# Another order for the mixer's 627 steps

## The chip, the core and the metric

The kernel runs on one core of one Trainium2 chip. The time is device microseconds of one launch. TensorE (PE) does the matmuls, VectorE (DVE), ScalarE (ACT) and GpSimd (POOL) work beside it, and SyncE (SP) issues most DMAs. Each engine takes its instructions in the order in which they are written for it, and waits on semaphores for what others produce.

## What is computed

One encoder layer on x of 512 positions by 1024 channels, in float32: a half-step FFN, a mixer of a Fourier part (512 channels) and grouped-query attention (8 query heads, 2 key heads of 64), and a second half-step FFN. The part that the change concerns:

```python
h = rms_norm(x, mix_norm)
u = h @ w_in                       # fourier 512 | q 8x64 | k 2x64 | v 2x64
f_out = fourier_mixer(u[..., :512], fnet_w, fnet_b)
    # Re(DFT2 over positions and a group's 128 channels), then a 128x128 map, 4 groups
a_out = gqa_attention(u_q, u_k, u_v, q_norm, k_norm)
    # per-head RMSNorm and axial rotary on q and k, softmax over all 512 keys
x = x + concat([f_out, a_out]) @ w_out
```

## The kernel before

**Stages.** FFN 1, the mixer and FFN 2 follow each other; in the profile the mixer's first matmul starts at 331.27 us and its last product ends at 491.05. Most matmul operands are split into a high and a low part, so that a product is three matmuls (high x high, high x low, low x high; L185 for the turned form). The high part (a step `.h`, or `h...`) is a cast, as a rule on ACT, the low part (`.l`, or `l...`, L129) a subtraction on DVE.

**The mixer as a list of steps.** Each step is a named closure that issues its instructions on its engines; the string ORDER names all 627, and L1393 to L1395 call them one after the other under a manual schedule, so each of the five engines gets its instructions in just that order. Nothing else decides it. The steps by name:

- `wk.r`, `wq0.r` to `wq3.r`, `wv.r`, `f0.r` to `f3.r`, `fw.r`, `o0.r` to `o7.r`: load a weight tile (SP, L153) into one of three raw buffers; `.h` (ACT, or DVE for f0 and f1; L840) and `.l` (DVE) split it.
- `k.0` to `k.7`, `q0.0` to `q3.7`, `v.0` to `v.7`: the projections, eight chunks of three matmuls each.
- For k and each q: `.sq` (ACT, squares), `.pq` (PE, four transposes, L917), `.s0`, `.s1` (sum and power), `.sw` (ACT, scaled copy, L877 or L882), `.sd` (q1 to q3 alone: four swap DMAs on SP, L891), `.rc`, `.rs` (DVE, the rotation), `.h`, `.l`. `kp` are four transposes on PE for k, `vt`, `vp`, `vs` bring v to rows (`vp`: four transposes, L983).
- `f<h><c>.0`, `.1`: the Fourier projections (twelve 256-column matmuls each, L1020 to L1022), with `.u`, `.e`, `.h`, `.l` behind them; `map0`, `map1`, `d..`, `c..` are the transforms. `pos` (L1391) issues three DMAs on POOL's queue with their tables.
- `s<t><c>` (PE, L1217): the scores of query pair t (two heads, b = 0 and 1) for query block c, into two PSUM banks. `m<t><c>` (DVE, L1226) takes the maxima, `e<t><b><c>` (ACT, L1243) the exponential into the head tile `th<t><b>`, `g` and `n<t><b><c>` (ACT, L1279) the scaling by the sum.
- The way to the transposed head blocks. For t = 1 to 3: `t<t><b><k>` (four transposes on PE, L1256), `h` (ACT, L1261) and `l` (DVE). For t = 0 (BY_BLOCKS): `T<t><b><g>` (DVE transposes 32x32 pieces), `Z<t><b><g>` (SP stores the piece to DRAM, L1162), `z<t><b><g>` (SP loads it back in another order, L1169), `h` (ACT, L1183), `l` (DVE). A block 00 or 01 has four of each.
- `v<t><b><k>` (PE, L1290): the attended sum, two matmuls; `o...c`, `o...a` and `r..` close a pair.
- `y<d>.0` to `.7` (PE): the output product; `y<d>.x` (DVE, L1328) adds it to x, `.q` squares it (ACT), `.a` adds that to the norm's sum (DVE, L1339), `.h`, `.l` scale and split it for FFN 2.

**What else binds the order.** Eight PSUM banks, mix0 to mix7 (L813), are handed out by `bank_for` in the order in which they were given back by `read`: a step that takes a bank waits for the last reader of its former content. Which bank a step gets therefore depends on ORDER too. The head tiles have two buffers: th10 and th11 take over those of the blocks 00 and 01, so the first exponential into each waits until that block's four stores are done. The loads `z` go into two `pt` buffers.

Of the kernel before, what the change touches and what calls it, by code (L numbers as in the profile page):

```python
# [50 lines left out]
ORDER = """
wq1.r wq0.r wk.r cos wk.h wk.l wq2.r k.0 k.1 wv.r wq0.h wq3.r k.2 k.3 k.4 k.5 k.6 wq0.l k.7 n1.c k.sq wq1.h n1.m q0.0
k.pq k.s0 wq1.l wq2.h q0.1 q0.2 q0.3 wq2.l q0.4 q0.5 k.s1 kw q0.6 k.sw q0.7 q0.sq k.rc q0.sw kp q1.0 q0.pq q2.0 q1.1
q1.2 k.rs km q1.3 q0.s0 q1.4 wv.h k.h q1.5 q0.rc q1.6 q0.rs q0.h k.l q1.7 q0.l f0.r s00 wv.l q1.sw s02 q0.s1 wq3.h
q1.sq m00 m02 f2.r s01 q2.1 m01 v.0 e010 e012 e000 q1.pq g00 q2.2 q1.s0 q2.3 e002 pos s03 v.1 g02 q2.4 q1.sd v.2 e011
v.3 e001 f1.r n012 n000 m03 wq3.l e013 q1.s1 e003 q3.0 v.4 v.5 n002 q1.rc q2.5 g01 g03 n001 n003 n011 q1.rs q2.6 v.6
n010 T000 q1.h Z000 q3.1 T002 q3.2 T003 Z002 n1.p v.7 q1.l q2.7 Z003 n013 T013 s13 s11 T012 T010 vt T011 f0.h Z010
q2.sq T001 Z011 f0.l m11 s10 Z012 q2.sw Z001 e101 Z013 m13 fw.r q3.3 f1.h e103 e111 z011 q3.4 f00.0 q3.5 z010 q3.6
e113 q2.sd m10 q3.7 f1.l f2.h z012 q2.rc q3.sq z003 vp z013 e100 q3.sw f2.l f01.0 vs s12 f00.1 h011 g13 f02.0 h010
z002 m12 f02.1 o0.r e110 v.h f01.1 f03.0 e112 z000 z001 q2.pq q2.rs v.l l010 q3.rc q2.h g11 e102 h000 q2.l v010 q3.pq  # L60
f00.u l000 v000 f02.e n103 l011 h002 f3.r n101 f12.0 g12 f03.1 h001 v011 f10.0 g10 l002 l001 q3.sd v001 q2.s0 n100
f01.u n112 q3.rs f3.h n102 v002 t100 n111 h012 f3.l l012 n113 f10.1 h003 f02.h h013 q3.s0 l003 t102 n110 h100 f10.u
v003 t101 f03.e h102 q2.s1 v012 l013 v013 f03.h l100 o00.c f02.l f12.1 h101 o01.c t110 h110 v100 l102 o00.a q3.h l101
t112 v101 f12.e t103 v102 h112 s22 h103 o01.a q3.l l112 o2.r s23 l103 fw.h f12.h m23 l110 r0.h t111 m22 h111 v103 e203
e213 f03.l l111 f11.0 fw.l t113 g23 e202 f11.1 f11.u s21 s20 o10.c v110 e212 n203 n213 m21 f13.0 e201 h113 f13.1 m20
d10 e211 f12.l g21 f13.e e200 o10.a g22 map0 o1.r n201 e210 d00 f13.h map0.h n202 d01 g20 d0.h map1 n200 map1.h l113
r0.l d11 f13.l v111 map0.l t202 d0.l map1.l t200 v112 d1.h d1.l s32 h202 h200 n210 o0.h c0.c c0.s l202 t201 c0.q q3.s1
l200 m32 v113 o0.l n212 d20 o11.c o1.h c0.o c1.s h201 c1.q c0.h d21 d2.h o3.r c1.c o11.a n211 c1.o d30 s33 l201 v200
t203 v201 d2.l o2.h h203 e312 t210 m33 l203 v202 d31 c0.l t213 h210 l210 e313 v203 t211 d3.h h213 t212 d3.l l213 h211
c1.h l211 s31 e303 e302 v210 o5.r v211 m31 c2.s h212 g33 e301 e311 s30 l212 v212 m30 n303 o2.l y0.0 c2.q c1.l n313  # L70
c3.s c2.c e300 g31 g32 v213 e310 o20.c o1.l n301 y2.0 g30 y2.1 c2.o y0.1 n302 n300 y1.0 c2.h y1.1 o20.a t302 t301 c3.c
c3.q t300 n312 h302 c2.l h300 c3.o c3.h l300 y2.2 c3.l n311 o21.c y1.2 t303 r1.h n310 o21.a y0.2 v300 y0.3 r1.l y2.3
h303 h301 l303 t310 y2.4 l301 r2.h o4.r t313 y0.4 v301 l302 v302 h310 t311 v303 l310 t312 v310 o7.r h313 y1.3 h311
l311 o30.c l313 h312 o6.r v311 l312 y2.5 v312 v313 y0.5 y1.4 r2.l o31.c o30.a y1.5 o31.a y1.6 r3.h y0.6 r3.l y0.7 y1.7
o5.h o5.l o3.h y2.6 y2.7 y0.x y5.0 y5.1 y5.2 o4.h o3.l y3.0 y5.3 y5.4 y5.5 y3.1 y3.2 o4.l y3.3 y0.h y3.4 y4.0 y3.5
y5.6 y3.6 y4.1 y5.7 y2.x y2.q y2.h o6.h y0.q y5.x y4.2 o6.l y3.7 y4.3 y6.0 y1.x y4.4 y2.l y1.q y6.1 y1.h o7.h y6.2
y3.x y4.5 y4.6 y6.3 o7.l y1.a y4.7 y6.4 y0.l y5.h y6.5 y4.x y5.q y4.h y3.q y6.6 y7.0 y4.q y7.1 y7.2 y2.a y1.l y3.h
y6.7 y4.l y7.3 y3.a y7.4 y5.l y6.x y3.l y4.a y7.5 y5.a y7.6 y6.h y6.q y7.7 y6.a y7.x y7.q y7.h y6.l y7.a y7.l
"""


# [1546 lines left out]
```

## Time and profile before

| | us |
|---|---|
| runs | 823.25, 826.04, 826.79 (median 826.04) |
| the profiled execution | 825.55 |
| its span, first to last instruction | 823.8 |
| mean granted TensorE clock | 0.994 of full speed |
| the mixer, first matmul to last | 331.27 to 491.05 |
| the mixer's stretch at half clock | 387.33 to 394.16 |

The profile comes from one execution, and all times in the trace are counted from the span's start. Names in it leave out buffer numbers: `mix` is one of the eight banks, `th` a head tile, `pt` a block that has come back from DRAM, `ph` and `pl` its high and low part, `sw_q` the swapped half of a query, `raw_f` a raw weight tile. In lists of waits, "PE mix L1290 <- ACT ph L1183" means that a matmul of line 1290 into a bank sat idle until the ACT instruction of line 1183, which writes `ph`, had ended.

### The profile page before, as it was taken

How to read it: one execution, taken by the hardware profiler on the slowest of the kernel's cores; microseconds unless marked ns; L12 is line 12 of the kernel's file. 1: busy time of each engine (PE TensorE's matmuls, PEld its weight loads, DVE VectorE, ACT ScalarE, POOL GpSimd, SP SyncE). 2: the span in 40 equal slices, each digit the busy share in tenths (PEclk: the TensorE clock that was granted, in tenths of full speed). 3: DMA queues.
4: the chain of work that ended last, by engine and by line, in shares of the span. 5: the costliest groups of instructions: out<-in, count | busy, mean ns of one | idle time of the engine just before them, and what ended most of it. 6: DMA issues, size and time to landing. Idle time of an engine off the chain costs nothing.

```text
span 823.8 us, 13012 instructions
## 1 busy us (share of the span) xinstructions
PE 811.9 (99%) x4936; PEld 723.8 (88%) x4936; DVE 649.3 (79%) x1065; ACT 499.7 (61%) x864; POOL 67.1 (8%) x75
## 2 busy tenths in 40 slices
PE   9999999999999999998999999999999999999997
PEld 7889998799989998877987888889988998899987
DVE  7997997489856857787898488999955998479674
ACT  7883774168524745677899467657732774257562
POOL 0320000000000100210100002200000100000001
PEclk9999999999999999999999999999999999999999
DMA  7874543345443423458011226564442553445222
GB/s 256 198 176 166 152 121 90 122 129 166 90 154 103 115 53 115 145 203 210 27 52 52 78 77 166 115 192 147 116 123 95 154 162 77 140 129 133 69 78 102
DMA packets 39838, 103.95 MB, mean 126 GB/s; under 512 B 4704, under 2 KB 10976, under 8 KB 39776
## 3 DMA queue, kind: packets, MB, share of 16 engines
q1 hardware_dynamic: 30080, 86.80, 32.7%
q0 software_dynamic: 8832, 15.34, 11.0%
q8 instruction: 38, 0.62, 0.3%
q10 hardware_dynamic: 864, 0.98, 0.3%
q14 instruction: 24, 0.20, 0.1%
HBM read 95.51 MB, written 4.19 MB: 121 GB/s over the span
## 4 chain that ended last, share of the span: by engine, by line
PE 87%; ACT 5%; DVE 4%; DMA 2%; issue 1%; POOL 0%; SPq 0%; POOLq 0%; DVEq 0%; ACTq 0%
PE dn L185 24%; PE r L435 12%; PE r L440 8%; PE gu L185 7%; PE mix L185 6%; PE q L435 4%; PE q L440 4%; PE r L431 4%; PE p L431 4%; PE q L431 4%; PE gu L739 3%; ACT th L1243 2%; PE p L440 2%; PE mix L1290 1%; ACT th L1279 1%
## 5 line engine op out<-in xcount | busy, mean ns | idle before, releaser
L185 PE MATMUL dn<-at,ring 128*128 128x512 f32 x900 | 202.9, 380 | 1.1 <-DVE ring L129 1.1
L185 PEld LDWEIGHTS dn<-at,ring 128*128 128x128 f32 x900 | 168.0, 188 | 30.1 <-DVE ring L129 1.5
L440 PE MATMUL r<-rt,ring 128*128 128x256 f32 x560 | 154.3, 276 | 0.0
L435 PE MATMUL r<-rt,ring 128*128 128x256 f32 x840 | 147.1, 276 | 0.0
L435 PEld LDWEIGHTS r<-rt,ring 128*128 128x128 f32 x840 | 127.1, 188 | 1.6
L440 PEld LDWEIGHTS r<-rt,ring 128*128 128x128 f32 x560 | 105.1, 188 | 0.2
L390 ACT CAST ring<-s 128x1024 fp32r<-128x1024 f32 x70 | 73.5, 1051 | 35.8 <-PE r L435 16.5
L129 DVE TENSOR_TENSOR ring<-s,ring 128x1024 fp32r<-128x1024 f32 x70 | 85.3, 1218 | 12.3 <-ACT ring L390 10.2
L574 DVE SCALAR_TENSOR_TENSOR gx<-dn,gx 128x512 f32<-128x512 f32 x61 | 41.9, 688 | 62.2 <-PE dn L185 62.1
L171 ACT CAST ring<-raw_dn 128x768 fp32r<-128x768 f32 (+3 forms) x58 | 45.3, 784 | 70.2 <-PE dn L185 55.3
L440 PE MATMUL q<-rt,ring 128*128 128x256 f32 x280 | 77.0, 275 | 0.0
L159 POOL DMA_DIRECT2D ring<-in_wgu x38 | 32.9, 866 | 470.7 <-ACT u L449 340.5
L129 DVE TENSOR_TENSOR ring<-raw_dn,ring 128x768 fp32r<-128x768 f32 (+3 forms) x58 | 51.5, 891 | 9.2 <-ACT ring L171 4.8
L440 PEld LDWEIGHTS q<-rt,ring 128*128 128x128 f32 x280 | 52.6, 188 | 0.0
L129 DVE TENSOR_TENSOR ring<-raw_g,ring 128x1024 fp32r<-128x1024 f32 x35 | 42.7, 1220 | 9.9 <-PE p L431 9.6
L435 PE MATMUL q<-rt,ring 128*128 128x256 f32 x280 | 49.8, 277 | 0.0
L185 PE MATMUL gu<-ring 128*128 128x512 f32 x216 | 48.9, 381 | 0.0
L431 PE MATMUL r<-rt,ring 128*128 128x512 f32 x140 | 48.6, 383 | 0.0
L431 PE MATMUL q<-rt,ring 128*128 128x512 f32 x140 | 48.4, 382 | 0.0
L431 PE MATMUL p<-rt,ring 128*128 128x512 f32 x140 | 48.3, 382 | 0.0
L185 PEld LDWEIGHTS gu<-ring 128*128 128x128 f32 x216 | 40.4, 188 | 6.9
L390 ACT CAST ring<-raw_g 128x1024 fp32r<-128x1024 f32 x35 | 36.8, 1051 | 14.0 <-DMA raw_g<-in_wgu 11.0
(276 smaller groups left out, 1636.7 us busy)
## 6 DMA issues: line engine op xcount, KB each, us to landing
raw_g<-in_wgu SPq DMA_DIRECT2D x35, 512.0 KB, 3.9
raw_u<-in_wgu SPq DMA_DIRECT2D x35, 512.0 KB, 4.5
raw_dn<-in_wd SPq DMA_DIRECT2D x40, 384.0 KB, 3.2
ring<-in_wgu POOLq DMA_DIRECT2D x35, 256.0 KB, 4.4
raw_gu<-in_wgu SPq DMA_DIRECT2D x12, 512.0 KB, 3.4
raw_o<-in_wo SPq DMA_DIRECT2D x8, 512.0 KB, 3.4
raw_dn<-in_wd SPq DMA_DIRECT2D x8, 448.0 KB, 3.4
raw_wq<-in_wins SPq DMA_DIRECT2D x4, 512.0 KB, 3.3
```

The costliest lines, as they stand in the source:

```text
L129: nc.vector.tensor_tensor(out=lo, in0=src, in1=asf(hi), op=ALU.subtract)
L159: nc.gpsimd.dma_start(out=lo, in_=src, accum_op=ALU.add)
L171: nc.scalar.copy(hi[:, :n, :], raw[:, :n, :])
L185: nc.tensor.matmul(ps, a, b, start=first and b is mhi and a is whi, stop=last and a is wlo)
L390: nc.scalar.copy(hi, src)
L431: nc.tensor.matmul(turned(ps), whi[:, ks], turned(m), start=start, stop=False, skip_group_check=True)
L435: nc.tensor.matmul(ps[:, t], whi[:, ks], m[:, o * HALF :][:, t], start=start and o == 0, stop=False, skip_group_check=True,)
L440: nc.tensor.matmul(o, wlo[:, ks], m, start=False, stop=stop, skip_group_check=True)
L574: nc.vector.scalar_tensor_tensor(out=x[d][:, t], in0=ps[:, t], scalar=0.5, in1=x[d][:, t], op0=ALU.mult, op1=ALU.add)
L739: nc.tensor.matmul(turned(pss[c]), w[:, k % 2, c], turned(m[k]), start=k == 0 and m is hh and w is hi, stop=k == KD - 1 and w is lo,)
L1243: nc.scalar.activation(prob[t, b, c], scores, AF.Exp, bias=mxs[n][:, b : b + 1], scale=f[:, b : b + 1], accum_out=zs[t][:, c, b : b + 1],)
L1279: op(f"n{t}{b}{c}")(lambda b=b: nc.scalar.activation(prob[t, b, c], prob[t, b, c], AF.Copy, scale=z(b)))
```

## The change

Only the string ORDER differs. It names the same 627 steps, in another order from its first line to its last; no step's own code changes. Its first two lines and the line with block 00's last store, before and after:

```diff
-wq1.r wq0.r wk.r cos wk.h wk.l wq2.r k.0 k.1 wv.r wq0.h wq3.r k.2 k.3 k.4 k.5 k.6 wq0.l k.7 n1.c k.sq wq1.h n1.m q0.0
-k.pq k.s0 wq1.l wq2.h q0.1 q0.2 q0.3 wq2.l q0.4 q0.5 k.s1 kw q0.6 k.sw q0.7 q0.sq k.rc q0.sw kp q1.0 q0.pq q2.0 q1.1
...
-n010 T000 q1.h Z000 q3.1 T002 q3.2 T003 Z002 n1.p v.7 q1.l q2.7 Z003 n013 T013 s13 s11 T012 T010 vt T011 f0.h Z010
...
+wk.r wk.h wq0.r wv.r wk.l k.0 k.1 k.2 wq1.r k.3 wq0.h k.4 k.5 k.6 k.7 wq0.l n1.c q0.0 wq2.r cos k.sq wq3.r k.pq q0.1
+q0.2 k.sw q0.3 q0.4 n1.m f1.r f2.r q0.5 k.s0 q0.6 k.rc wq1.h wq1.l wq2.h q0.7 k.s1 kw kp q0.sw k.rs q1.0 q1.1 wq2.l
...
+Z002 q3.5 T000 q3.6 T012 vt s13 s10 Z013 Z012 T011 f1.h q2.rc m13 e103 s11 q3.7 Z000 m11 f1.l m10 q3.sw Z010 q3.sq
```

What this does to the engines is shown at three places. First SP's queue around the stores Z (out, L1162) and the loads z (pt, L1169) of the blocks 00 and 01; sw is the four swaps `.sd`, raw a weight load. A row is line, operation, what it writes and reads, and how often in a row. Before:

```order
L153 DMA raw_f2_3479<-in_winf 128x1024
L891 DMA sw_q1_3458<-own_q1_3459 32x512 x4
L153 DMA raw_f1_3545<-in_winf 128x1024
L1162 DMA out00_3588<-th00_3501 128x512 x3
L1162 DMA out01_3628<-th01_3498 128x512 x3
L1162 DMA out00_3588<-th00_3501 128x512
L1162 DMA out01_3628<-th01_3498 128x512
L153 DMA raw_fw_3658<-in_fw 128x512
L1169 DMA pt01_3667<-out01_3628 32x4x512 x2
L891 DMA sw_q2_3646<-own_q2_3647 32x512 x4
L1169 DMA pt01_3667<-out01_3628 32x4x512
L1169 DMA pt00_3710<-out00_3588 32x4x512
```

And SP after:

```order
L153 DMA raw_f0_3529<-in_winf 128x1024
L153 DMA raw_f3_3570<-in_winf 128x1024
L891 DMA sw_q2_3584<-own_q2_3585 32x512 x4
L1162 DMA out00_3622<-th00_3506 128x512 x3
L1162 DMA out01_3649<-th01_3511 128x512 x2
L1162 DMA out00_3622<-th00_3506 128x512
L1162 DMA out01_3649<-th01_3511 128x512 x2
L1169 DMA pt01_3721<-out01_3649 32x4x512 x4
L1169 DMA pt00_3780<-out00_3622 32x4x512 x2
L891 DMA sw_q3_3682<-own_q3_3683 32x512 x4
L153 DMA raw_fw_3848<-in_fw 128x512
L1169 DMA pt00_3780<-out00_3622 32x4x512 x2
```

The swaps of q2 moved from behind the stores to ahead of them, block 00's fourth store from seventh to sixth place, and the eight loads now follow the stores directly, with the swaps of q3 and fw ahead of the last two.

Second, ACT around the first exponentials of pair 1 (th10 and th11; mix are the banks of their scores, own_q2 and own_q3 the copies `.sw`). Before:

```order
L976 COPY vt_3624<-mix5_3293 128x512
L869 ACTIVATE sq_q2_3630<-mix7_3295 128x512
L877 ACTIVATE own_q2_3647<-mix7_3295,qkg_119 128x512
L1243 ACTIVATE th10_3651,z1_3650<-mix6_3294,mx11_3635,sc_3287 128x512
L1243 ACTIVATE th10_3651,z1_3650<-mix0_3288,mx13_3654,sc_3287 128x512
L1243 ACTIVATE th11_3665,z1_3650<-mix1_3289,mx11_3635,sc_3287 128x512
L1243 ACTIVATE th11_3665,z1_3650<-mix2_3290,mx13_3654,sc_3287 128x512
L840 CAST more_3283<-raw_f2_3479 128x1024
```

After:

```order
L877 ACTIVATE own_q2_3585<-mix7_3295,qkg_119 128x512
L1279 ACTIVATE th01_3511<-th01_3511,z0_3505 128x4x4x32 x2
L869 ACTIVATE sq_q2_3611<-mix7_3295 128x512
L976 COPY vt_3635<-mix3_3291 128x512
L1243 ACTIVATE th10_3661,z1_3660<-mix2_3290,mx13_3656,sc_3287 128x512
L877 ACTIVATE own_q3_3683<-mix4_3292,qkg_119 128x512
L869 ACTIVATE sq_q3_3686<-mix4_3292 128x512
L1243 ACTIVATE th11_3688,z1_3660<-mix6_3294,mx13_3656,sc_3287 128x512
L840 CAST more_3283<-raw_f2_3376 128x1024
```

The first exponential of pair 1 is now e103, reading mix2, and not e101; q3's copy and squares stand between it and the second one.

Third, PE where f00.0 (the first Fourier projection) ends. Before, the projection chunk q3.5 and vp follow:

```order
L1020 MATMUL mix7_3295<-ring_61 128x256
L1021 MATMUL mix7_3295<-ring_61 128x256
L1022 MATMUL mix7_3295<-ring_61 128x256
L185 MATMUL mix3_3291<-ring_61,more_3283 128x4x32x4 x9
L983 MATMUL mix6_3294<-ident_108,vt_3624 128x128 x4
```

After, f02.0 follows:

```order
L1020 MATMUL mix3_3291<-ring_61 128x256
L1021 MATMUL mix3_3291<-ring_61 128x256
L1022 MATMUL mix3_3291<-ring_61 128x256
L1020 MATMUL mix2_3290<-ring_61 128x256
L1021 MATMUL mix2_3290<-ring_61 128x256
```

The projection q3 is now finished ahead of f00.0, vp comes behind f03.0, and the step behind f00.0 takes mix2, the bank that e103 reads.

More of the change, by code (lines that the diff above doesn't have):

```diff
@@ L51 @@
 ORDER = """
-wq1.r wq0.r wk.r cos wk.h wk.l wq2.r k.0 k.1 wv.r wq0.h wq3.r k.2 k.3 k.4 k.5 k.6 wq0.l k.7 n1.c k.sq wq1.h n1.m q0.0
-k.pq k.s0 wq1.l wq2.h q0.1 q0.2 q0.3 wq2.l q0.4 q0.5 k.s1 kw q0.6 k.sw q0.7 q0.sq k.rc q0.sw kp q1.0 q0.pq q2.0 q1.1
-q1.2 k.rs km q1.3 q0.s0 q1.4 wv.h k.h q1.5 q0.rc q1.6 q0.rs q0.h k.l q1.7 q0.l f0.r s00 wv.l q1.sw s02 q0.s1 wq3.h
-q1.sq m00 m02 f2.r s01 q2.1 m01 v.0 e010 e012 e000 q1.pq g00 q2.2 q1.s0 q2.3 e002 pos s03 v.1 g02 q2.4 q1.sd v.2 e011
-v.3 e001 f1.r n012 n000 m03 wq3.l e013 q1.s1 e003 q3.0 v.4 v.5 n002 q1.rc q2.5 g01 g03 n001 n003 n011 q1.rs q2.6 v.6
@@ L57 @@
-n010 T000 q1.h Z000 q3.1 T002 q3.2 T003 Z002 n1.p v.7 q1.l q2.7 Z003 n013 T013 s13 s11 T012 T010 vt T011 f0.h Z010
[L58 to L76, printed above, removed]
@@ L77 @@
-y3.x y4.5 y4.6 y6.3 o7.l y1.a y4.7 y6.4 y0.l y5.h y6.5 y4.x y5.q y4.h y3.q y6.6 y7.0 y4.q y7.1 y7.2 y2.a y1.l y3.h
-y6.7 y4.l y7.3 y3.a y7.4 y5.l y6.x y3.l y4.a y7.5 y5.a y7.6 y6.h y6.q y7.7 y6.a y7.x y7.q y7.h y6.l y7.a y7.l
+wk.r wk.h wq0.r wv.r wk.l k.0 k.1 k.2 wq1.r k.3 wq0.h k.4 k.5 k.6 k.7 wq0.l n1.c q0.0 wq2.r cos k.sq wq3.r k.pq q0.1
+q0.2 k.sw q0.3 q0.4 n1.m f1.r f2.r q0.5 k.s0 q0.6 k.rc wq1.h wq1.l wq2.h q0.7 k.s1 kw kp q0.sw k.rs q1.0 q1.1 wq2.l
+q1.2 km q0.rc q1.3 k.h q1.4 k.l q1.5 q0.sq q0.rs q0.pq q1.6 wv.h q0.s0 q2.0 q0.h q1.7 q0.s1 q0.l wv.l wq3.h s00 q1.sw
@@ new lines @@
+m00 s01 s02 m01 q2.1 q2.2 q2.3 q1.sq q1.sd m02 wq3.l e000 q2.4 e010 q2.5 s03 g00 q1.rc e001 q2.6 f0.r e011 q2.7 g01
+e002 m03 e012 v.0 q1.pq n000 n011 n001 e013 q3.0 q3.1 q1.rs v.1 e003 g02 f0.h g03 f0.l n010 f3.r n002 q1.s0 n003 v.2
+q1.h T002 v.3 q2.sw n013 q1.l T001 T003 q3.2 n012 T013 q3.3 v.4 v.5 q1.s1 n1.p q2.sd q2.sq v.6 q3.4 v.7 Z001 T010 Z003
+Z002 q3.5 T000 q3.6 T012 vt s13 s10 Z013 Z012 T011 f1.h q2.rc m13 e103 s11 q3.7 Z000 m11 f1.l m10 q3.sw Z010 q3.sq
+e113 f00.0 q2.rs Z011 q3.rc f02.0 f2.h g13 z013 z010 e111 f00.1 f03.0 f2.l vp e101 e110 q3.pq vs z011 e100 z012 s12
@@ new lines @@
+h011 h012 v.h m12 v.l z001 l011 h010 f02.1 z003 g10 f00.u e112 q2.pq f01.0 q3.sd e102 l010 f02.e n110 f10.0 n100 v010
+v011 f3.h fw.r g11 z002 z000 n101 f03.1 q2.h q3.rs h013 q2.s0 h000 l012 f12.0 n103 g12 f3.l f01.1 l000 n113 q2.s1 n102
+q3.s0 f01.u v012 f03.e h002 o5.r t101 v000 n111 l013 t100 h001 q2.l f10.1 fw.h f03.h f10.u v013 l001 l002 f12.1 v001
+h003 v002 q3.h f03.l fw.l l003 f12.e t102 n112 h100 h101 l101 l100 o2.r v003 o01.c o00.c s22 s23 h102 o00.a o01.a v100
+l102 v101 pos t103 m22 t110 r0.h f02.h f11.0 h103 m23 f11.1 h110 e212 f12.h f11.u t112 f02.l v102 l103 e213 l110 t113
@@ new lines @@
+t111 h112 e203 o0.r v103 q3.l l112 s21 g23 e202 s20 f13.0 o10.c f13.1 n203 m21 h113 e211 o10.a map1 e201 m20 o2.h l113
+v110 e200 e210 o2.l d00 map1.h g21 f13.e o1.r map1.l n201 map0 h111 map0.h g22 d01 g20 d10 l111 d11 d0.h n202 d0.l
+v111 v112 n200 d1.h f13.h t200 v113 c0.s map0.l f12.l d1.l h200 c1.c f13.l o11.c c0.c c1.s c0.q l200 q3.s1 c0.o t201
+n210 o11.a d20 t202 n212 o3.r c1.q h201 d21 h202 c1.o n213 t203 d2.h v200 l201 l202 s33 h203 s32 d2.l n211 v201 l203
+c2.s t212 c0.h o0.h m33 m32 d30 d31 e313 t211 h212 c2.q d3.h c0.l e312 v202 h211 l212 c2.c v203 t210 t213 d3.l c2.o
@@ new lines @@
+s31 l211 h210 l210 c3.s m31 v210 e302 o0.l c1.h v211 c3.q c1.l s30 m30 o1.h v212 e311 e303 e301 y0.0 c2.h o1.l o6.r
+o4.r g31 g32 e310 h213 e300 l213 c2.l c3.c y0.1 g33 g30 y2.0 n301 n302 n303 y2.1 y1.0 y1.1 v213 r0.l y0.2 y2.2 y1.2
+n300 t301 c3.o t300 o20.c t302 o20.a t303 c3.h n311 c3.l y1.3 h300 y0.3 h301 n313 l300 h302 v300 l302 l301 h303 n310
+y1.4 y2.3 v301 n312 o21.c t310 o21.a h310 y2.4 t311 l310 t312 v302 t313 r1.h l303 r2.h v303 r1.l h311 v310 l311 v311
+h312 h313 o30.c l312 y0.4 l313 v312 o30.a v313 r2.l o31.c y2.5 o31.a y0.5 y2.6 r3.h y1.5 r3.l y1.6 y2.7 o5.h y1.7 y0.6
@@ L79 @@
+o5.l y0.7 y0.x y5.0 y5.1 o3.h o7.r y5.2 o3.l y3.0 y2.x y2.h y5.3 y2.q y3.1 y1.x y3.2 y5.4 y3.3 y2.l y5.5 y5.6 o6.h
+y5.7 y3.4 o4.h y1.h o4.l y3.5 y3.6 y3.7 y1.q y4.0 o6.l y0.q y5.x y4.1 y6.0 y3.x y6.1 y4.2 y4.3 y0.h o7.h y1.a y5.q
+y6.2 y4.4 y4.5 y2.a y6.3 y3.q y4.6 y4.7 o7.l y4.x y5.h y3.a y6.4 y1.l y4.q y0.l y6.5 y4.a y3.h y6.6 y6.7 y5.l y7.0
+y7.1 y6.x y7.2 y5.a y6.h y3.l y7.3 y6.l y6.q y7.4 y6.a y7.5 y4.h y7.6 y7.7 y7.x y4.l y7.q y7.a y7.h y7.l
 """
```

## The prediction

> **What bounds the kernel now.** I read the page's busy times first, then PE's list of waits, then PE's timeline at the longest wait, then the stretches around it.
>
> ```profile
> PE 811.9 (99%) x4936; PEld 723.8 (88%) x4936; DVE 649.3 (79%) x1065; ACT 499.7 (61%) x864; POOL 67.1 (8%) x75
> PE mix L1290 <- ACT ph L1183: 1.9, 1, 1.9
> PE mix L917 <- ACT th L1243: 1.2, 1, 1.2
> PE mix L1256 <- ACT th L1279: 0.5, 1, 0.5
> ```
>
> TensorE is busy for 811.9 of 823.8 us and has three waits of note (columns: total us, times, longest). All three lie in the mixer, which is the only stage that the change reorders; both FFNs keep their order. So the change can win what PE loses in the mixer, and no more, and it can lose whatever new waits it makes. The largest loss stands here:
>
> ```profile
> 383.73 0.60 PE L917 MATMUL mix<-ident,sq_q 128*128 128x128 f32 x4
> 384.59 0.49 PE L1290 MATMUL mix<-ph,near 128*128 128x512 f32 x1 [0.26 <-DVE near L129]
> 385.19 0.49 PE L1290 MATMUL mix<-pl,near 128*128 128x512 f32 x1
> 385.52 0.60 PE L917 MATMUL mix<-ident,sq_q 128*128 128x128 f32 x4
> 387.98 0.79 PE L1290 MATMUL mix<-ph,near 128*128 128x512 f32 x1 [1.86 <-ACT ph L1183]
> ...
> 337.65 0.60 PE L917 MATMUL mix<-ident,sq_k 128*128 128x128 f32 x4
> 338.00 4.90 PE L185 MATMUL mix<-ring 128*128 128x512 f32 x21
> ```
>
> Each row is start, length, instruction, and in brackets the idle time ahead and who ended it. The last two rows give unhindered rates: four transposes take 0.35 us start to start, and a 512-column matmul (4.90 - 0.38) / 20 = 0.226. From 383.73 to 387.98 PE did 2 x 0.35 + 2 x 0.226 = 1.15 us of work in 4.25 us: **3.1 us are lost** while v010 and v000 wait for the head blocks that return from DRAM. Then the clock falls:
>
> ```profile
> 387.98:394.16 6.18, 6.18 (x25) 5.65 (x26) 6.10 (x13) 6.18 (x11) 1.92 (x1) 0.50 0.05 13
> 394.16:400.00 5.84, 5.84 (x46) 5.47 (x45) 4.11 (x8) 3.97 (x8) 1.84 (x2) 1.00 0.27 91
> ```
>
> In the table by stretches (PE first, the granted clock third from the right) PE does 25 matmuls in 6.18 us at clock 0.50 and then 46 in 5.84 us at 1.00. At the later rate the 25 take 3.2 us: **another 3.0 us** that the wait left behind. The 1.2 us wait (q1.pq, 354.70) did not cost clock. So what the mixer can give back is about 1.2 + 3.1 + 3.0 + 0.5 = 7.8 us, under 1%.
>
> **What goes.** q1.pq now stands behind q2.7 and v.0, when the exponentials that hold its bank have long read it: -1.2. The head blocks' way (e, n, T, store Z, load z, h) ends earlier against PE: in the new order v010, v000 and their kin stand behind more f-products, and the loads z are no longer mixed with o0.r and f3.r. I follow them with rows:
>
> ```profile
> L1162 SPq DMA_DIRECT2D out<-th x5: 320/320/443, 367.4 to 369.5; - x5
> DMA to landing us min/median/max: 2.0/2.4/2.9
> L1169 SPq DMA_DIRECT2D pt<-out x8: 302/442/580, 370.7 to 377.7; - x8
> DMA to landing us min/median/max: 4.4/5.6/9.5
> 371.75 2.42 SPq L891 DMA_DIRECT2D sw_q<-own_q  x4
> ```
>
> The first of five stores issued at 367.4 lands 2.0 later, the last at 369.5 + 2.9 = 372.4: 0.75 us apart, so they queue up: the issues are 0.53 apart. The first of the eight loads lands at 370.7 + 4.4 = 375.1 and the last at 377.7 + 9.5 = 387.2; between them land seven loads, one weight load (o0.r) and four swaps, which I count as one since they are as large as one load: 12.1 / 9 = 1.34 each. In the new order all eight stores have landed by about 376 (worked out below); then come eight loads, four swaps and fw, ten times 1.34: the last load lands near 389.4. From e103 (at 374.6, below) to h000 ACT has 22 instructions, by these groups (count, busy time, mean ns):
>
> ```profile
> L1243 ACT ACTIVATE th<-mix,mx,sc 128x512 f32<-128x512 f32 x32 | 24.8, 783 | 4.8 <-DVE mx L1227 4.3 <-PE mix L1256 0.5
> L1279 ACT ACTIVATE th<-th,z 128x512 f32<-128x512 f32 x32 | 22.3, 728 | 0.0
> L840 ACT CAST ring<-raw_o 128x1024 fp32r<-128x1024 f32 x5 | 5.2, 1043 | 0.0
> L1183 ACT CAST ph<-pt 128x512 fp32r<-128x512 f32 x8 | 4.8, 616 | 5.4 <-DMA pt<-out 3.0 <-issue 1.4 <-PE mix L1290 1.0
> ```
>
> 8 exponentials (6.3), 4 steps h (2.5), 3 scalings (2.2), f2.h and f3.h (2.1), and 5 of some 0.6 (3.0) make 16.1 us; so ACT comes to h000 near 390.5, and PE to v000 after 392. Both waits go: **-3.1, and -3.0 with the clock**. The wait ahead of t302 goes too (-0.5: y0.0 to y2.1 and the scalings are re-dealt there). At the end:
>
> ```profile
> 487.59 3.46 PE L185 MATMUL mix<-near,ring 128*128 128x512 f32 x15
> 489.54 2.21 DVE L1339 TENSOR_TENSOR acc<-acc,sq 128x512 f32<-128x512 f32 x3
> 491.67 0.68 DVE L1328 TENSOR_TENSOR gx<-mix,gx 128x512 f32<-128x512 f32 x1
> ```
>
> The last product ends at 491.05, but y7.x starts at 491.67, behind three square sums that the new order does earlier. FFN 2's norm hangs on y7.x: -0.6. Sum of what goes: **-8.4 us**. If the cover fails (the last load lands after 391.5), v000 waits again; that is a rival below. I cost two moves at nothing: the step pos (three transfers on POOL's queue, at 348 in before) now starts near 390, behind the loads, and its first reader map1 stands some 20 us further on; and the first weight loads wk, wq0 and wv on SP's queue land beside FFN 1's last down products, as wq1, wq0 and wk did.
>
> **What comes.** The new place to wait is f02.0, the PE step that in the new order follows f00.0. It takes the PSUM bank of score block s13, which e103, the first exponential of query pair 1, frees on ACT. e103 writes a head buffer that is free only when block 00 has been stored: four stores, and the last of them, Z000, is the sixth of eight in SP's queue. Ahead of the stores SP now issues the four swaps q2.sd. In the order of before those stood behind the stores, and PE had q3.3 to q3.7 to do meanwhile. The rows:
>
> ```profile
> 349.72 1.22 DVE L129 TENSOR_TENSOR ring<-raw_wv,ring 128x1024 fp32r<-128x1024 f32 x1
> 352.48 1.28 ACT L1243 ACT_TABLE_LOAD   x1 [0.58 <-DVE mx L1227]
> 353.78 0.78 ACT L1243 ACTIVATE th<-mix,mx,sc 128x512 f32<-128x512 f32 x1
> 361.06 3.19 ACT L1279 ACTIVATE th<-th,z 128x512 f32<-128x512 f32 x5
> 364.12 0.63 ACT L939 CAST near<-rot_q 128x512 fp32r<-128x512 f32 x1
> 367.57 0.68 ACT L877 ACTIVATE own_q<-mix,qkg 128x512 f32<-128x512 f32 x1
> 371.85 0.78 ACT L1243 ACTIVATE th<-mix,mx,sc 128x512 f32<-128x512 f32 x1 [3.59 <-DVE mx L1227]
> 374.34 0.36 PE L1020 MATMUL mix<-ring 128*128 128x256 f32 x1
> ```
>
> - The first exponential started at 353.78. Its maximum m00 comes about 0.8 us later now, because k.sw and wq1.h stand on ACT ahead of what DVE needs, and DVE idles there and does wq2.l afterwards, a lows step of the length of wv.l here; bounds 0 and 1.2. So 354.6.
> - From there to q1.h ACT needed 364.12 - 353.78 = 10.34 for 8 exponentials and 7 scalings. Now 6 scalings precede it, one less at 3.19 / 5 = 0.64: 9.7. With q1.h 0.63 and q2.sw 0.68, q2.sw ends at 365.6.
> - SP needs 2.42 for q2.sd: the first store goes out at 368.1, the sixth 5 x 0.38 later at 370.0 (issues took 0.32 to 0.44).
> - The first lands 2.1 after its issue, at 370.2, the sixth 5 x 0.75 later at **374.0**; with the swaps still in the queue up to 375.2.
> - e103 takes 0.78: f02.0 can start at 374.8 to 376.0; I take 375.4.
> - PE arrives there earlier. In before it began f01.0 at 374.34, having done the same work plus vp (0.35) and waited 1.2, so 372.8; with fewer changes between kinds of matmul a little less, with new short waits ahead of kp, q0.pq and s00 (taken as 0.9, between 0 and q1.pq's 1.2) a little more: 373.0, give or take 0.5.
>
> So f02.0 waits **+2.4 us** (1.3 to 3.5), and ACT idles some 6 us ahead of e103. Behind e103 on ACT stand q3.sw, q3.sq, e113 and f2.h: f03.0, q3.pq and the exponentials of pair 1 wait with it. The clock then is at stake. It fell after idle of 0.26 and 1.86 us close together, and not after 1.2; at 2.4 I take it to fall and to cost what it cost before: **+3.0** (0 to 3.4). Short waits: kp, q0.pq, s00 +0.9; further down t101, s23, t200 and t210, where ACT's or DVE's durations, laid end to end along the new order, end 0.5, 0.9, 0.6 and 0.4 behind PE's: 2.4 in all. A PE that runs 3 us late at half clock swallows the first two, so +1.0 (0 to 2.4). Sum of what comes: **+7.3 us**.
>
> **Sum.** -8.4 + 7.3 = -1.1. The profiled run took 825.55 us, 1.75 more than its span, and lies 0.5 under the median of 826.04, inside the runs' 823.25 to 826.79. 825.55 - 1.1 = **824.5 us**: the wait and its half clock move from v000 to f02.0.
>
> The Trainium skill, "TensorE: Matmul & The Clock Gate", section "What's actually happening", lets the clock fall only after at least one idle window of about 3.4 us. By that rule f02.0's wait would leave the clock alone and the sum would be that of the first rival. This trace speaks against it: the clock fell after a longest idle stretch of 1.86 us.
>
> **Rivals.**
> 1. *The clock stays up behind f02.0.* If the wait is short (1.3) or split by the end of the stretch over which activity is counted, the 3.0 go, and t101 and s23 wait again (+1.4): 824.5 - 3.0 + 1.4 = 822.9. For it: 1.2 us was harmless. Against it: 1.86 was not. 17%.
> 2. *The new order does what a search with the right transfer times should:* block 00 lands in time and f02.0 hardly waits: 824.5 - 2.4 - 3.0 + 1.4 = 820.5. It needs the six stores to land by 372, so 0.36 apart; five of before's were 0.75 apart. 10%.
> 3. *Slower: two long waits.* The last load lands after 391.5, because loads, swaps and fw share the queue after the stores: 2 us later than I add up, as z001 did here when swaps came between (9.5 us from issue). Then h000, l000 and v000 wait as in before, some 1.5 us, and the clock falls a second time (+3.0): 829.0. The point is 391.5, and PE, slowed at f02.0, is likelier to be late itself. 9%.
> 4. The remaining 64% is the forecast, within 822.5 to 827.
>
> **How the numbers follow.** A measurement here tells about 0.5% (4.1 us) from no change. Faster by more: the second rival, a part of the first, and a new f02.0 wait at its lower bound, 0.18. Slower by more: part of the third and what I don't see, 0.09. Same: 0.73. The range takes in the first and second rival at the low end (820.5) and most of the third at the high end (828.5).
>
> **What would show it.** Right: PE's longest wait is f02.0 (L1020) for an exponential (ACT th L1243), ACT idles 5 to 7 us ahead of it, a stretch at 0.50 follows it, and v010 and v000 (L1290) wait for nothing. Wrong: f02.0 without a wait (the stores landed sooner), a full clock behind it, or L1290 waiting for ph L1183 as before. A PE wait at k.0 or map1 would show that the moves costed at nothing were not free.

## The result, and the profile after

The change makes the kernel faster, by more than was forecast: 817.78 us (817.47 to 818.53, 4 runs) against 825.15 (823.25 to 826.79, 4 runs), ratio 0.9913, 95% interval 0.9888 to 0.9938. On the chip of e5 the ratio was 0.9929 (0.9915 to 0.9942). One execution of before on that chip took 1680.56 us, twice the others, and no comparison uses it. The forecast was 824.5, in a range of 820.5 to 828.5, with 0.18 on faster: the time lies below the range.

The profiled execution took 818.53 us with a span of 816.8, 7.0 under the span of before. Its list of PE's waits (total us, times, longest):

```profile
PE dn L185 <- DVE ring L129: 1.0, 1, 1.0
PE busy L684 <- PEq L1611: 0.8, 1, 0.8
PE mix L1020 <- ACT th L1243: 0.7, 1, 0.7
PE gu L739 <- ACT ring L725: 0.4, 1, 0.4
PE mix L1256 <- ACT th L1279: 0.3, 1, 0.3
```

Of the mixer's waits two are left, L1020 (f02.0, as predicted, but 0.7 and not 2.4) and L1256 (t200, 0.3). L1290 behind ph and L917 behind th are gone. The chain ahead of f02.0, in the timelines of SP, ACT and PE (start, length, instruction, idle ahead):

```profile
365.59 2.41 SPq L891 DMA_DIRECT2D sw_q<-own_q  x4
368.10 4.67 SPq L1162 DMA_DIRECT2D out<-th  x8
...
353.31 1.28 ACT L1243 ACT_TABLE_LOAD   x1 [0.75 <-DVE mx L1227]
354.61 0.78 ACT L1243 ACTIVATE th<-mix,mx,sc 128x512 f32<-128x512 f32 x1
373.89 0.78 ACT L1243 ACTIVATE th<-mix,mx,sc 128x512 f32<-128x512 f32 x1 [5.00 <-DMA out<-th]
...
372.61 0.28 PE L1020 MATMUL mix<-ring 128*128 128x256 f32 x1
373.88 0.28 PE L1022 MATMUL mix<-ring 128*128 128x256 f32 x1
374.81 0.39 PE L1020 MATMUL mix<-ring 128*128 128x256 f32 x1 [0.66 <-ACT th L1243]
```

The swaps go ahead of the stores, ACT idles 5.0 us for a store, and then e103 lets f02.0 start: every link of the prediction up to there is found, with other sizes. e103 starts at 373.89, and PE comes to f02.0 near 374.0, one step of 0.11 behind the last matmul of f00.0. The half clock that was to follow does not come, and the stretch in which before had it runs at full speed (PE first, granted clock third from the right):

```profile
373.97:380.00 6.03, 5.37 (x46) 5.04 (x44) 5.91 (x12) 6.03 (x14) 0.00 (x0) 1.00 0.99 245
387.00:394.00 7.00, 7.00 (x59) 6.74 (x58) 6.22 (x14) 6.99 (x13) 5.35 (x5) 1.00 0.60 184
```

v000 starts straight behind t101, with no idle time in brackets, and y7.x 0.2 us behind the last product, which ends at 484.53:

```profile
391.06 0.60 PE L1256 MATMUL mix<-ident,th 128*128 128x128 f32 x4
391.41 0.48 PE L1290 MATMUL mix<-ph,near 128*128 128x512 f32 x1
...
331.94 1.26 PE L185 MATMUL mix<-ring 128*128 128x512 f32 x5
483.27 1.26 PE L185 MATMUL mix<-near,ring 128*128 128x512 f32 x5
484.10 0.69 DVE L1339 TENSOR_TENSOR acc<-acc,sq 128x512 f32<-128x512 f32 x1
484.70 0.69 DVE L1328 TENSOR_TENSOR gx<-mix,gx 128x512 f32<-128x512 f32 x1
```

From its first matmul to the end of its last product the mixer took 484.53 - 331.94 = 152.6 us, against 491.05 - 331.27 = 159.8 before: 7.2 less. It began 0.7 later, since FFN 1, whose code is the same, ended later in this execution. In the profiled executions of this study, which come from several chips, the mixer began between 329.8 and 332.7 us, so single executions are compared below by the mixer's length.

### The profile page after: what moved, and what is told of

The parts are those of the page before. It is cut to its first block, busy times and chain, and to the rows that moved or that the text cites. A ratio compares the mean times of both kernels' runs of the same rounds, so it can differ in the third digit from the quotient of the medians.

```text
span 816.8 us, 13024 instructions
## 1 busy us (share of the span) xinstructions
PE 808.2 (99%) x4936; PEld 722.0 (88%) x4936; DVE 648.5 (79%) x1065; ACT 498.7 (61%) x864; POOL 66.6 (8%) x75
## 4 chain that ended last, share of the span: by engine, by line
PE 91%; DVE 3%; ACT 3%; DMA 1%; issue 1%; POOL 0%; POOLq 0%; DVEq 0%
PE dn L185 24%; PE r L435 12%; PE r L440 8%; PE gu L185 8%; PE mix L185 6%; PE q L435 4%; PE q L440 4%; PE r L431 4%; PE q L431 4%; PE p L431 4%; PE gu L739 3%; PE p L440 2%; PE mix L1290 2%; PE mix L1256 1%; ACT th L1243 1%
## 5 line engine op out<-in xcount | busy, mean ns | idle before, releaser
L185 PE MATMUL dn<-at,ring 128*128 128x512 f32 x900 | 202.8, 380 | 1.0 <-DVE ring L129 1.0
L185 PEld LDWEIGHTS dn<-at,ring 128*128 128x128 f32 x900 | 167.9, 188 | 30.0 <-DVE ring L129 1.4
L185 PE MATMUL gu<-ring 128*128 128x512 f32 x216 | 48.9, 381 | 0.0
L185 PEld LDWEIGHTS gu<-ring 128*128 128x128 f32 x216 | 40.4, 188 | 6.9
```

What stands on the lines that cost most here:

```text
L185: nc.tensor.matmul(ps, a, b, start=first and b is mhi and a is whi, stop=last and a is wlo)
```

## The experiments

Each is an edit of ORDER alone, so all of them compute the same. In an edit the line with "-" is the stretch of ORDER as it was and the line with "+" the same stretch as it became; both are shortened, and "..." stands for steps left out. Comparisons are with before on the same chip: e1 to e4 ran on one chip, e5 to e8 on a second, e9 to e11 on a third. "Clock" is an execution's mean granted clock: 6.8 us at half clock cost 0.004, 3.4 us cost 0.002, and the last microseconds of the kernel, which run at half clock in every profiled execution, up to 0.002. So 0.999 and above means no half clock inside the kernel, 0.997 and below some, and 0.998 most likely none.

### e1: before, one weight load behind two loads of blocks

```diff
-z002 m12 f02.1 o0.r e110 v.h f01.1 f03.0 e112 z000 z001 q2.pq
+z002 m12 f02.1 e110 v.h f01.1 f03.0 e112 z000 z001 o0.r q2.pq
```

> The order of before with one step moved: the weight load o0.r goes behind the loads z000 and z001 on SP's queue. Theory A (the half clock of before is set off by the long wait at v000, so that wait and clock go together): the load took 1.4 us of the queue ahead of z000 and z001, so the last block lands near 385.8 instead of 387.2, v000 starts some 1.4 us earlier, its longest wait falls from 1.9 to about 0.5, the clock stays at 1.00 and the mixer gains 1.4 + 3.0: about 820.8 us, mean clock 0.999. Theory B (the half clock has another cause, or comes from the summed idle of the whole mixer): only 1.4 us, about 823.7, mean clock 0.994 as before. Theory C (the wait moves on to the next step that hangs on ACT): no gain, 825.

Measured: 820.44 against 822.66, ratio 0.9975 (0.9965 to 0.9985), and a clock of 0.998 to 1.000 in all nine executions, where before on this chip had 0.994 to 0.996 in four of twelve. In the profile the wait at v000 is down to two short ones:

```profile
383.10 0.48 PE L1290 MATMUL mix<-ph,near 128*128 128x512 f32 x1 [0.23 <-DVE near L129]
384.93 0.49 PE L1290 MATMUL mix<-ph,near 128*128 128x512 f32 x1 [0.30 <-ACT ph L1183]
385.65 0.50 PE L1290 MATMUL mix<-pl,near 128*128 128x512 f32 x1 [0.24 <-DVE pl L129]
```

The mixer took 155.9 us, 3.9 less than in the profiled execution of before, where theory A had 4.4. A late load of one block is indeed what PE waits for, and in these nine executions the half clock went with the wait. It did not go for good: e10, which keeps this move, had a clock of 0.997 in two of ten, and its profile shows a half clock behind waits of 1.0 and 0.3 at v010 and v000. That the median gains 2.2 and not 4.4 has a reason that the executions of before show (the list of executions under e5 to e7): before's half clock comes in part of them only.

### e2, e3, e4: after, the store Z000 later and earlier

```diff
-vt s13 s10 Z013 Z012 T011 f1.h q2.rc m13 e103 s11 q3.7 Z000 m11 ... q2.rs Z011 q3.rc
+vt s13 s10 Z013 Z012 T011 f1.h q2.rc m13 e103 s11 q3.7 m11 ... q2.rs Z011 Z000 q3.rc
```

> The order of after with one step moved: the store Z000 goes from sixth to eighth place among the eight stores. The eighth store landed 1.6 us behind the sixth in the trace of after, so e103 and f02.0 start some 1.6 us later and f02.0 waits about 2.4 us, which is what the prediction gave it. Theory A (a wait of that length costs half a clock stretch): 817.8 + 1.6 + 3.0 = 822.4, mean clock 0.995, a stretch at 0.50 behind f02.0. Theory B (the clock stays up): 817.8 + 1.6 = 819.4 or a little less where later short waits take it up, mean clock 0.999.

In e3 Z000 stands behind z010 instead:

> The order of after with Z000 behind the loads z013 and z010, which themselves wait for stores to land: Z000 is issued near 374.2 and lands near 377.6, so f02.0 waits about 4.5 us. Theory A: the clock falls, 817.8 + 3.7 + 3.0 = 824.5 with mean clock 0.995 or lower. Theory B (no fall below a whole idle stretch of about 3.4 us counted from a fixed grid): the fall comes in some runs only, 821.5 or 824.5.

In e4 it stands behind Z002, and T000 behind T003:

> The order of after with Z000 two places earlier in SP's queue (fourth of eight) and T000 earlier on DVE to serve it. Z000 lands near 372.4 instead of 373.8, e103 then waits for its maximum m13 alone and starts near 372.9. If the wait at f02.0 costs time: f02.0 starts within 0.2 us of the end of f00.0 and the time falls by 0.7 to 0.8, to 817.0. If the steps behind it on PE are themselves bound by ACT and DVE: s12 and t101 wait instead and the time stays at 817.8.

Measured, against the same 822.66: e2 817.72, ratio 0.9938 (0.9923 to 0.9953); e3 818.82, 0.9953 (0.9938 to 0.9968); e4 816.99, 0.9930 (0.9915 to 0.9945). Mixer 153.2, 154.9 and 152.5 us. The clock was 0.998 or more in eleven of twelve executions, and 0.997 in one of e3, its slowest (819.2). f02.0, in e2, e3 and e4:

```profile
374.24 0.39 PE L1020 MATMUL mix<-ring 128*128 128x256 f32 x1 [1.35 <-ACT th L1243]
...
373.78 0.39 PE L1020 MATMUL mix<-ring 128*128 128x256 f32 x1 [2.21 <-ACT th L1243]
...
372.10 0.39 PE L1020 MATMUL mix<-ring 128*128 128x256 f32 x1 [0.28 <-ACT th L1243]
```

The waits came out shorter than was meant, because e103 does not wait for Z000 in either e2 or e3. In e3 it starts at 372.86, 0.66 us after the issue of Z000 (the second row), which landed 3.9 us after its issue. What lets it start is the store of the first row, block 01's last, which landed 3.3 us after its issue:

```profile
369.47 0.60 SPq L1162 DMA_DIRECT2D out<-th  x1
...
372.20 0.42 SPq L1162 DMA_DIRECT2D out<-th  x1
...
372.86 0.78 ACT L1243 ACTIVATE th<-mix,mx,sc 128x512 f32<-128x512 f32 x1 [6.46 <-DMA out<-th]
```

In e2 it is the same: the seventh store, issued at 370.23 and landed 3.0 us later, lets e103 start at 373.32, while Z000 landed at 374.2. So with Z000 last, th10 takes the buffer of the block that is stored first, 01; both expectations had overlooked this. What follows all the same: by their mean clock, waits of 1.35 and 2.21 us at f02.0 left the clock up in seven of eight executions, so theory A (the prediction's) found little support at these sizes. And e4 shows that f02.0's wait of 0.7 is worth little by itself: it went down to 0.28, and f02.0 started 0.9 us earlier against the mixer's first matmul, but the mixer is as long as after's (152.5 against 152.6). Behind s12, which now waits 0.17, PE is only 0.3 ahead, and at t100 0.1.

### e5, e6, e7: after again, and with e103 held back on DVE

e6 moves m13 and e103 behind f1.l, e7 behind m10:

```diff
-f1.h q2.rc m13 e103 s11 q3.7 Z000 m11 f1.l m10 q3.sw
+f1.h q2.rc s11 q3.7 Z000 m11 f1.l m13 e103 m10 q3.sw
```

> The kernel of after, unchanged, as the reference on this chip for the next two. On the chip of the first four experiments before took 822.7 where it had taken 825.2, so after should stand near 817 beside it, ratio 0.991 to 0.994.

> The order of after with m13 and e103 behind m11 and f1.l: DVE does 2.8 us of other work first, e103 starts some 1.4 us later by the trace of after (375.3 instead of 373.9) and f02.0 waits for it by 2.1 to 2.4 us, the size that the prediction gave it. Theory A (the prediction's: such a wait fells the clock and costs 3.0 more): 1.4 + 3.0 over after, 821.4 where after is 817.0, mean clock 0.996 or lower. Theory B (the half clock needs most of one 3.4 us stretch of a free-running grid to be idle, and a single wait of 2.4 mostly misses that): 818.4, mean clock 0.998 to 1.000 in most executions, since a wait of this size is often cut in two by the end of a stretch.

> As e6, but m13 and e103 behind m10 as well: e103 starts 2.8 us later than in after and f02.0 waits some 3.6 us. Theory A: 2.8 + 3.0 over after: 822.8 where after is 817.0, mean clock 0.996 or lower in nearly every execution. Theory B: the share of executions with a half clock rises: with 3.6 idle us one stretch of 3.4 us always holds 1.8 of them or more, so about half to all of the executions fall; 819.8 without the fall, 822.8 with it. Theory C (only a wholly idle stretch counts): hardly any fall, 819.8.

Measured: before 823.42; e5 816.98, ratio 0.9929 (0.9915 to 0.9942), mixer 152.9 us where after's first profile has 152.6; e6 819.73, 0.9961 (0.9949 to 0.9973); e7 821.37, 0.9981 (0.9972 to 0.9990). The waits at f02.0, in e6 and in e7:

```profile
PE mix L1020 <- ACT th L1243: 3.0, 1, 3.0
...
PE mix L1020 <- ACT th L1243: 4.4, 1, 4.4
```

The executions, time and clock:

```
e5      816.4 .998  816.6 .999  817.0 .999  817.3 .999  817.3 .998
e6      818.0 .999  818.2 .998  818.2 .998  818.5 .999  818.8 .999
        819.7 .996  819.8 .997  820.1 .996  820.3 .995  820.8 .997  821.0 .995  822.1 .995
e7      820.8 .997  820.9 .995  821.2 .997  821.2 .997  821.3 .996  821.4 .997
        821.5 .995  821.9 .997  822.1 .995  822.5 .995  822.9 .995
before  at .999 and above: 821.3 to 822.2 (5 executions);  at .994: 823.9 to 824.8 (6);
        17 others between, 821.9 to 824.3
```

One program has two outcomes. Five executions of e6 kept the clock and took 818.3 on average, 1.3 over after; seven lost some of it and took 820.5. e7 lost it in all eleven. Before itself has both ends: 821.3 to 822.2 with the full clock, 823.9 to 824.8 with the lowest. The profiled execution of before, at 0.994, is like the latter. The clock is not all that differs, though: among the 17 others, nine at 0.998 took from 821.9 to 824.2.

Where the difference lies can be read from the starts of the half clock. In every profile the granted clock changes only at whole multiples of 3.413 us from its last change: in before it is full for 382.29 us (112 of them), half for 6.83 (2) and full for 426.67 (125). This grid of stretches does not follow the program: in before, e6 and e7 a stretch ends 1.4, 2.6 and 3.1 us behind the mixer's first matmul. In the profile of before the half clock lasts 2 x 3.41 us, and in e7 as well (374.77 to 381.59, 6.82). Counted back from its start in steps of 3.41, the stretch ahead of it held this, in before, then e7, each with the stretch that follows:

```profile
383.92:387.33 3.41, 1.82 (x10) 0.98 (x8) 2.48 (x5) 1.96 (x6) 0.00 (x0) 1.00 1.03 266
387.33:390.74 3.41, 2.77 (x9) 2.23 (x10) 2.79 (x8) 3.41 (x7) 0.00 (x0) 0.50 0.22 54
...
371.35:374.77 3.42, 1.04 (x10) 0.84 (x8) 3.28 (x7) 0.00 (x0) 0.00 (x0) 1.00 0.99 328
374.77:378.18 3.41, 1.36 (x6) 1.37 (x7) 2.92 (x6) 2.29 (x5) 0.00 (x0) 0.50 1.04 226
```

PE was busy for 1.82 and 1.04 us of 3.41, and the clock fell at the end of the stretch, although in before it had no idle time longer than 1.86 and in e7 the wait went on for another 2 us. Theory C (only a wholly idle stretch counts) is excluded by both. Theory A's "such a wait fells the clock" is right for 7 of 12 executions at 3.0 us. Theory B fits best: what PE does in one stretch of 3.4 us decides, and where the stretches begin differs from execution to execution, so that a wait of 3.0 falls within one stretch or is cut in two, while one of 4.4 always takes 2.2 us or more out of some stretch. That this is what parts e6's two outcomes is argued, since only one of its executions has a profile. PE's busy time is not the measure: in that profile, which kept the clock, the stretch that ends at 373.56 (counted back from the half clock at the kernel's end) held less of it than before's:

```profile
370.15:373.56 3.41, 1.50 (x13) 1.30 (x11) 3.27 (x7) 0.00 (x0) 0.00 (x0) 1.00 1.01 346
```

The next column, the busy time of the weight loads (PEld), does sort the stretches: 0.98 and 0.84 us ahead of the two falls above and 1.11 ahead of e10's (last section), against 1.30 here. Counted over this grid in all thirteen profiles (from 8 us on), the falls at the kernel's end included, no stretch ahead of a fall held more than 1.11 us of weight loads, and no other one at full clock held less than 1.30. The number of matmuls that start in a stretch sorts them as well (8 at most, 9 at least), so what the clock follows stays open.

### e8: before with e1's move and q1.pq later

```diff
-e010 e012 e000 q1.pq g00 q2.2 q1.s0 q2.3 e002 pos s03 v.1 g02 q2.4
+e010 e012 e000 g00 q2.2 q2.3 e002 pos s03 v.1 q1.pq g02 q1.s0 q2.4
```

> The order of before with the move of e1 (o0.r behind z000 and z001) and one more: q1.pq behind v.1 and q1.s0 behind g02, so that PE does not wait 1.2 us for the exponentials that hold its bank. Theory A (a wait that is removed is time won): 1.2 less than e1, which was 2.2 under before: ratio near 0.996. Theory B (PE's place there is bound by the exponentials on ACT, not by the one step): the wait moves to s03 and q3.0, which take the next banks, and the time is that of e1, ratio 0.9975, or longer.

Measured: 821.36 against 823.42, ratio 0.9979 (0.9971 to 0.9987), mixer 156.3 us where e1 had 155.9: nothing won over e1. PE's waits from 345 to 400 us:

```profile
PE mix L185 <- DVE more L129: 1.0, 1, 1.0
PE mix L1290 <- ACT ph L1183: 0.3, 1, 0.3
PE mix L1290 <- DVE pl L129: 0.2, 1, 0.2
PE mix L1217 <- ACT th L1243: 0.2, 1, 0.2
```

The wait for th (L917, 1.2) is gone, and 0.2 at s03 (L1217) and 1.0 at q3.0 (L185, for the low part of q3's weights) have come: theory B as to the outcome, but the second wait is for DVE, which does wq3.l late, and not for a bank as expected. In the order of after wq3.l stands ahead of e000, and no wait for it is in the list.

### e9: before with v010 and v000 later

```diff
-q2.l v010 q3.pq f00.u l000 v000 f02.e n103 l011 h002 f3.r n101 f12.0 g12 f03.1 h001
+q2.l q3.pq f00.u l000 f02.e n103 l011 h002 f3.r n101 f12.0 g12 f03.1 v010 v000 h001
```

> The order of before with v010 and v000 behind f03.1 on PE, loads and ACT unchanged. PE has f12.0 and f03.1 (2.8 us) to do while the blocks come back, so the long wait at v000 should go. Theory A (PE follows ACT and DVE there, so the waits stay in sum and spread over f12.0, v011, t100 and f10.1, by 0.7 to 1.0 each; but no stretch is idle enough for the clock): mean clock 0.998 or more in nearly every execution, the time of before's executions at full clock (821.3 to 822.2), ratio 0.998. Theory B (the wait is simply filled): 3 us less in every execution, under 819.5, ratio 0.995. Theory C (spread waits fell the clock as well): ratio 1.000 and clocks of 0.994 to 0.996 as often as in before.

Measured: 823.99 against 824.35, ratio 0.9999 (0.9988 to 1.0010), clock 0.998 to 1.000 in all eleven executions; before had 0.997 or less in 12 of 21 there. PE's waits from 345 to 400 us:

```profile
PE mix L917 <- ACT th L1243: 1.2, 1, 1.2
PE mix L1290 <- DVE pl L129: 0.8, 2, 0.7
PE mix L1256 <- ACT th L1279: 0.7, 1, 0.7
PE mix L1022 <- DVE ring L129: 0.4, 1, 0.4
```

The waits did spread, over v011, t100 and f10.1, and the clock stayed up, as theory A has it; theory B (filled by other work) is excluded. But the time did not fall by what the clock should give: theory A's ratio of 0.998 lies outside the interval. In the profiled execution the mixer took 157.3 us, 2.5 less than in before's, and yet the medians agree. Part of the answer lies in before's own executions on this chip: six with the full clock (0.999 and above) took 822.9 to 824.9, 823.7 on average, and the twelve at 0.997 and below 824.4. A half clock goes with only 0.7 us more here, where the ends on e5's chip lie 2.4 apart, and e9 takes what before takes here at full clock. Why the half clock costs so little on this chip stays open; both programs scatter by 3 to 4 us on it (822.5 to 826.6 and 822.9 to 825.7).

### e10: e1 with the square sum y6.a behind y7.x

```diff
-y7.6 y6.h y6.q y7.7 y6.a y7.x y7.q
+y7.6 y6.h y6.q y7.7 y7.x y6.a y7.q
```

> The order of e1 with one more move: the square sum y6.a behind y7.x on DVE. Theory A (the prediction's: FFN 2 hangs on y7.x): y7.x starts 0.2 us behind the last product y7.7 instead of 0.6, and the stretch from y7.7 to FFN 2's first matmul is 0.4 to 0.5 shorter; in the time 0.5 under e1, ratio 0.997, too little to tell in runs, so the trace decides. Theory B (FFN 2 hangs on the norm's sum, which still needs y6.a and y7.a): y7.x is earlier and FFN 2 is not; ratio 0.9975 as e1.

Measured: 822.13 against 824.35, ratio 0.9976 (0.9965 to 0.9987), as e1. y7.x starts 0.04 us behind the last product's end at 487.82, and FFN 2 gains nothing: from its first matmul to the norm's sum (ss) pass 5.17 us, against 496.03 - 490.89 = 5.14 in before and 489.00 - 484.37 = 4.63 in after. PE in e10, in before, in after:

```profile
487.66 4.80 PE L185 MATMUL gu<-ring 128*128 128x512 f32 x21
492.83 1.02 PE L243 MATMUL ss<-ones,acc 128*128 128x2 f32 x8 [0.37 <-DVE acc L1339]
...
490.89 4.80 PE L185 MATMUL gu<-ring 128*128 128x512 f32 x21
496.03 1.02 PE L243 MATMUL ss<-ones,acc 128*128 128x2 f32 x8 [0.34 <-DVE acc L1339]
...
484.37 4.80 PE L185 MATMUL gu<-ring 128*128 128x512 f32 x21
489.00 1.03 PE L243 MATMUL ss<-ones,acc 128*128 128x2 f32 x8
```

Theory B: FFN 2 hangs on the last square sum, which has all of DVE's work ahead of it, wherever y7.x stands. After is 0.5 better because one sum fewer is left at that point.

### e11: after with the swaps behind the stores

```diff
-q1.s1 n1.p q2.sd q2.sq v.6 ... q3.sw Z010 q3.sq
+q1.s1 n1.p q2.sq v.6 ... q3.sw Z010 q2.sd q3.sq
```

> The order of after with the four swaps q2.sd behind the seventh store on SP, as before had them behind the stores. Theory A (the swaps' 2.4 us ahead of the stores make e103 late, as the prediction has it): Z000 lands near 372.4 or earlier by after's trace, e103 then waits for its maximum alone (372.9), f02.0's wait of 0.7 falls to 0.2 or less; the time is 816.5 to 817, or that of after where q3.pq and s12 take the wait up. Theory B (e103 is bound by something else): f02.0 waits 0.7 as before the move.

Measured: 818.07 against 824.35, ratio 0.9929 (0.9917 to 0.9941), the ratio of after. e103 starts at 371.93, and f02.0 waits for nothing. But the time goes elsewhere, as ACT's timeline and PE's waits from 376 us on show:

```profile
371.93 0.78 ACT L1243 ACTIVATE th<-mix,mx,sc 128x512 f32<-128x512 f32 x1 [4.04 <-DVE mx L1227]
373.86 0.69 ACT L877 ACTIVATE own_q<-mix,qkg 128x512 f32<-128x512 f32 x1 [1.05 <-DMA sw_q<-own_q]
...
PE mix L1256 <- ACT th L1279: 0.9, 1, 0.9
PE mix L1217 <- ACT th L1243: 0.3, 1, 0.3
```

q3's copy writes the one buffer `own` that the swaps of q2 read, so ACT stands still 1.05 us until they have landed, and the exponentials behind it, then s12 and t101 on PE, are late (mixer 153.7 us). Theory A, as to the cause: the swaps' place is what makes e103 late in after. It is also what keeps q3's copy on time.

## Why the prediction was wrong

**The bound and what goes: right.** The prediction had 8.4 us to win, and each of its terms is gone from the profile of after: q1.pq, the waits of v010 and v000, the half clock, t302 and the tail. The two moves costed at nothing left no wait at k.0 or map1 in the list. The last product ends 7.2 us earlier against the mixer's start, and FFN 2's norm another 0.5. Of the 7.2, e1 gives 3.9 in its profile with one moved load. The rest is read from the profile of after and not shown by an edit: e8 removed q1.pq's wait and won nothing, and e9 spread v000's and won nothing. The tail's size was right and its reason was not: not y7.x but the square sum bounds it (e10).

**The last loads: right, with room.** v000 followed t101 without idle time, so the third rival did not happen. The last load landed at 388.2, where 389.4 was forecast.

**f02.0's wait: right in place and cause, mis-sized.** This is the first term that failed: "f02.0 waits +2.4 us (1.3 to 3.5)" measured 0.66 of idle time, 0.8 between the end of f00.0's steps and the start. Two parts of the sum made it so. "m00 comes about 0.8 us later" was 0.16 against the mixer's start: the first exponential started at 354.61, as forecast, but in an execution whose mixer began 0.67 later. The swaps did not delay the stores in the queue: the last began at 367.4 and was 2.3 us on the way at most (the row below), so it landed by 369.7, and the first store, issued at 368.1, landed 2.2 us later at 370.3; the first stores of before took 2.0 to 2.2. Together e103 came at 373.89 - 0.67 = 373.2 against the mixer's start, where 374.6 was taken: 0.6 of the difference is m00, 0.6 the allowance for swaps in the queue. PE's arrival was within its bounds: 374.0 - 0.67 = 373.3, where 373.0 give or take 0.5 was said, and took another 0.3 off the wait. The swaps' times from issue to landing:

```profile
L891 SPq DMA_DIRECT2D sw_q<-own_q x4: 513/582/589, 365.6 to 367.4; - x4
DMA to landing us min/median/max: 2.0/2.0/2.3
```

**"At 2.4 I take it to fall and to cost what it cost before: +3.0": wrong, and the larger error.** At 0.66 the clock stayed up, which is the first rival's condition, a short wait. But the step was wrong as a rule too: a wait of 2.2 (e3) brought the half clock in one of four executions, one of 3.0 in seven of twelve, one of 4.4 in all eleven (the waits as each one's profiled execution has them). Had f02.0 waited as long as forecast, the half clock would have been a matter of where the stretch of 3.4 us began, in perhaps no more than half the executions. The same holds for the 3.0 on the other side: before's own half clock is in part of its executions, and the profile happened to show one. On e5's chip the five executions of before at full clock took 821.3 to 822.2: against those, after's 817.0 is some 4.8 us of waits and nothing of clock. The price was too high as well: before's lowest clock goes with 2.4 us more than its full clock on that chip, and e6's seven that lost clock took 2.2 more than its five that kept it.

**The Trainium skill's rule on the clock** ("TensorE: Matmul & The Clock Gate", "What's actually happening"), that it falls only after at least one idle window of about 3.4 us, was set aside because of the 1.86 us in before. The window's length agrees with the half clocks of 3.41 and 6.83 us, and that it runs free of the program, as the page says too, with the different places of the stretches in before, e6 and e7. If idle means idle from end to end, that part does not agree: the clock fell behind stretches with PE busy for 1.82 and 1.04 of 3.41 us. Its result for f02.0, no fall, was the right one.

**Short waits: too dear.** 0.9 for kp, q0.pq and s00 and 1.0 for t101, s23, t200 and t210 were added; the list of waits has 0.3, at t200.

**The rivals.** The second rival's price, 820.5, is near the outcome, for another reason than its own: the stores did not land by 372 (e103 started at 373.9, right behind block 00's last one, issued at 370.8 and 3.0 us on the way), but PE came nearly as late. With 0.8 for f02.0, none for the clock and 0.3 for the short waits, the prediction's own sum is 825.55 - 8.4 + 1.1 = 818.3; the profiled execution took 818.53. So close an agreement is partly luck: 0.7 us of that time is FFN 1's later end, and e8 and e9 show that the terms do not simply add up.

## What to carry over

A half clock that one profile shows is a property of that execution; before it is put into a sum, look at the clocks of several executions, and count it by the share that has it. A removed wait counts as won only when the next step's operands are there: e4, e8 and e11 each removed or shortened one and lost the gain again at later steps, while the new order as a whole took 7 us off the mixer. When two chains meet, as the store and f00.0 did at f02.0, the forecast rests on the difference of two sums; take both from the same starting point (here the mixer's first matmul) and let the range follow their difference.
